# Loading every second expert tile from ScalarE's DMA queue in a mixture-of-experts decoder layer

## The chip, the cores and the metric

The kernel runs on one core of a Trainium2 chip. The metric is the device time of one execution in microseconds (us). The engines are named as in the profile: PE is TensorE's matmul, PEld its weight load, DVE VectorE, ACT ScalarE, POOL GpSimd, SP SyncE. SP computes nothing here; it issues loads and stores.

## The reference

One decoder layer for 256 tokens of width 1024 in float32. A combined projection feeds a Mamba-2 branch and a sliding-window attention branch; their gated sum is projected, added to the input and normalized to h. Then comes the part that the change touches, a layer of 32 experts of which each token uses 4:

```python
logits = xt @ w_router + b_router
top_logits, top_idx = lax.top_k(logits, 4)
gate_w = softmax(top_logits)
# for every expert e, over the tokens xb that chose it:
hgu = xb @ w_gate_up[e] + b_gate_up[e]          # (1024 x 2048) weights, 8 MB
glu, lin = split(hgu);  glu = min(glu, 7);  lin = clip(lin, -7, 7)
act = glu * sigmoid(1.702 * glu) * (lin + 1)
y   = act @ w_down[e] + b_down[e]                # (1024 x 1024) weights, 4 MB
out[t] = sum over the 4 experts of gate_w * y;   result = layer_norm(alpha * h + out)
```

## The kernel before, in words

**The stream.** All large weights are one list of 1 MB tiles, `stream` (line 85), in the order in which they are used. The first S_E = 50 belong to the projections; from there on come 32 x 12 = 384 expert tiles, which this document numbers 0 to 383. For expert e there are eight tiles "u" (gate and up weights) and four tiles "d" (down weights); the d tiles of an expert come after the u tiles of the next one (lines 177 to 183). So from e = 1 on, u of expert e are tiles 12e-4 to 12e+3, d of expert e are tiles 12e+16 to 12e+19. Each tile is read once and used for one group of matmuls.

**Buffers and the order of the loads.** A tile goes into one of NGRAN = 21 granules of 1 MB. One granule holds the normalized h (`hn`) to the end; in the expert stage the others rotate among the tiles, so that a load waits until the PE has finished the tile some 20 earlier. `weights(i)` calls `prefetch(i + 1 + st["ahead"])` (line 127), which writes the load instructions of all tiles up to `ahead` tiles further into the program, on SP. In the expert stage `ahead` is 17, and from tile 296 on (u of expert 25, line 1167) it is 6. Each load also reuses one of eight landing semaphores in turn, so it waits until the load eight before it has landed: at most eight tiles are in flight. SP executes its loads in program order and waits in front of each for its two conditions.

**One expert on the engines.** The loop at line 1159 goes over the tiles ("slots"). At each slot first the due events with pre=True run (`fire(n, True)`), then `weights`, then the tile's matmuls, then the events with pre=False. For expert e:

- after its last u tile, one slot later: ACT and DVE copy the two PSUM banks (`gu`, lines 992 and 994), the PE transposes the copies behind that slot's matmuls (`tu`, line 1004), DVE adds biases and clips, ACT takes the silu (`hg`, line 1015), DVE multiplies (`ac`). The result is needed 12 slots later;
- during the d tiles: the PE transposes gates (line 1041), ACT copies them (`S`);
- after its last d tile, one slot later: ACT copies the bank (`y`, line 1059), and behind that slot's matmuls the PE adds gates times y into the output banks (`out`, line 1054);
- for every second expert the PE gathers the token columns for two further experts in two units, and ACT copies each (`xg`).

**The branch.** After u of expert 27 (tile 327) `overflow()` (line 1063) reads a count from memory and enters a loop only if an expert has more than 64 tokens, which it has not with these inputs. Every engine takes the branch by itself.

**The end.** After tile 383 the last y and out follow, then a normalization on DVE with `lnd` (two loads of 512 KB behind the stream) and four stores. The last tile is loaded in two halves (line 105).

Of the kernel before, what the change touches and what calls it, by code (L numbers as in the profile page):

```python
# [45 lines left out]
def hybrid_layer(ctx, tc, x, w_in, conv_w, conv_b, dt_bias, a_log, d_skip, norm_w, w_ssm_out,  # L46
                 sinks, w_attn_out, b_gates, w_mix, ln1_g, ln1_b, w_router, b_router,
                 w_gate_up, b_gate_up, w_down, b_down, ln2_g, ln2_b, out, cap=CAP):
    nc = tc.nc
# [5 lines left out]
    def gtile(name, dt=F):  # L55
        return gran.tile([P, 2048], dt, name=name, tag="g")
# [39 lines left out]
    def prefetch(upto):  # L96
        while st["dma"] < min(upto, len(stream)):
            i = st["dma"]
            ap, nb = stream[i]
            t = gtile(f"raw{i}")  # L100
            t3 = t.rearrange("p (k n) -> p k n", n=nb)
            if len(halves(i)) > 1:
                nk = 2048 // nb // 2
                for k in (slice(0, nk), slice(nk, 2 * nk)):
                    nc.sync.dma_start(t3[:, k], ap[:, k])
            else:
                nc.sync.dma_start(t3, ap)  # L107
            raws[i] = t
            st["dma"] += 1

    def halves(i):

        return [slice(0, 1024), slice(1024, 2048)] if i in (0, len(stream) - 1) else [slice(0, 2048)]
# [11 lines left out]
    def weights(i):  # L125

        prefetch(i + 1 + st["ahead"])
        if i >= S_E:
            return raws.pop(i).rearrange("p (k n) -> p k n", n=1024)
        split_ahead(i)  # L130
        nb = stream[i][1]
        return tuple(t.rearrange("p (k n) -> p k n", n=nb) for t in splits.pop(i))
# [42 lines left out]
    S_E = len(stream)  # L175
# [30 lines left out]
    for c in range(2):  # L206
        nc.sync.dma_start(xn3[:, c], x[0, c * P:(c + 1) * P])
    prefetch(2)
    wdt = w1([P, KD, 32], "wdt")
    nc.sync.dma_start(wdt, w_in[0, :, OFF_DT:OFF_DT + 32].rearrange("(k p) n -> p k n", p=P))  # L210
# [692 lines left out]
    mix(1, 1)  # L903
    resid(1, 0)
    prefetch(S_E + MB)
    mix(1, 2)
    mix(1, 3)
# [326 lines left out]
```

## Time and profile before

| | |
|---|---|
| runs | 1333.29 us median of 3 (1332.5 to 1334.1) |
| profiled execution | 1332.57 us, span of the trace 1330.7 us |
| granted TensorE clock, mean | 0.988 |
| busy | PE 94%, DVE 32%, ACT 21%, POOL 5% of the span |
| DMA | 463.30 MB, mean 348 GB/s, all data loads on one queue |

Times in the rows are us from the start of the span. Busy time alone doesn't tell the bound: the rows to look at are what the PE and the load queue wait for, stage by stage. The expert stage runs from about 350 us to the end.

### The profile page before, as it was taken

To read this page: it belongs to the slowest core of one execution; us is meant where nothing else is said; L and a number is where in the kernel's file an instruction comes from. 1 tells how busy PE (TensorE), PEld (TensorE's weight loads), DVE (VectorE), ACT (ScalarE), POOL (GpSimd) and SP (SyncE) were. 2 spreads that over 40 slices of the span, in tenths; PEclk is the share of its full clock that TensorE was granted. 3 is DMA by queue.
4 is the path that set the end of the run, shared out by engine and by line. 5 is a ranking of instruction groups with operands and counts; after the bars stand their busy time and mean duration, and the time that the engine had idled before them with its cause. 6 is when DMAs were issued, how large, how long until landed. Compare 5 with 4: busy or idle time off the path is not lost. (4 is left out here: it accounts for less than half of the span.)

```text
span 1330.7 us, 16492 instructions
## 1 busy us (share of the span) xinstructions
PE 1252.8 (94%) x6864; PEld 668.4 (50%) x6864; DVE 431.6 (32%) x818; ACT 281.4 (21%) x477; POOL 63.1 (5%) x35
## 2 busy tenths in 40 slices
PE   7999999999999999999999989899898989879985
PEld 7998878999864344343342323333232323333221
DVE  6998987565632111211121111111111111111113
ACT  5555555543211111110011101001010101000001
POOL 0044332000000000000000000000000000000000
PEclk9999999999989999999999999999999999989998
DMA  9523334655999999999999999999999999989995
GB/s 300 182 64 104 118 123 147 207 185 187 355 420 421 421 421 422 421 421 420 421 421 421 422 421 420 421 421 421 421 421 421 422 421 421 421 352 421 420 420 235
DMA packets 106227, 463.30 MB, mean 348 GB/s; under 512 B 9948, under 2 KB 48996, under 8 KB 56964
## 3 DMA queue, kind: packets, MB, share of 16 engines
q1 hardware_dynamic: 106148, 462.19, 86.9%
q8 instruction: 57, 0.93, 0.3%
q14 instruction: 22, 0.18, 0.0%
HBM read 461.11 MB, written 1.05 MB: 347 GB/s over the span
## 5 line engine op out<-in xcount | busy, mean ns | idle before, releaser
L76 PE MATMUL u<-raw,xg 128*64 128x512 f32 x2048 | 470.1, 598 | 32.7 <-DMA raw<-in_w_gate_up_dram 32.6
L76 PEld LDWEIGHTS u<-raw,xg 128*64 128x64 f32 x2048 | 136.8, 136 | 335.1 <-issue 231.8
L76 PE MATMUL d<-raw,ac 128*64 128x512 f32 x1024 | 246.4, 607 | 17.6 <-DMA raw<-in_w_down_dram 11.1
L992 DVE COPY gu<-u 128x512 f32<-128x512 f32 x32 | 22.1, 692 | 708.4 <-PE u L76 708.4
L76 PEld LDWEIGHTS d<-raw,ac 128*64 128x64 f32 x1024 | 67.2, 137 | 147.0 <-issue 103.2
L65 DVE TENSOR_TENSOR wlo<-raw,whi 128x2048 fp32r<-128x2048 f32 (+1 forms) x51 | 120.4, 2371 | 13.3 <-ACT whi L62 11.4
L76 PE MATMUL ws<-xh,whi 128*128 128x256 f32 x400 | 102.1, 293 | 1.8 <-ACT whi L62 1.8
L62 ACT ACTIVATE whi<-raw 128x2048 fp32r<-128x2048 f32 (+1 forms) x51 | 95.4, 1874 | 27.6 <-DMA raw<-in_w_in_dram 8.0
L76 PE MATMUL ws<-xl,whi 128*128 128x256 f32 x400 | 98.7, 284 | 0.0
L62 ACT ACTIVATE gu<-u 128x512 f32<-128x512 f32 x32 | 19.1, 597 | 336.1 <-PE u L76 336.1
L76 PEld LDWEIGHTS ws<-xh,whi 128*128 128x128 f32 x400 | 77.2, 193 | 4.3 <-ACT whi L62 2.2
L76 PEld LDWEIGHTS ws<-xl,whi 128*128 128x128 f32 x400 | 77.3, 193 | 0.9 <-issue 0.7
L76 PEld LDWEIGHTS xg<-G,xr 128*128 128x128 f32 x512 | 62.4, 199 | 24.9 <-issue 24.3
L76 PE MATMUL xg<-G,xr 128*128 128x128 f32 x512 | 68.6, 289 | 0.2 <-DVE G L65 0.2
L62 ACT ACTIVATE xg<-xg 128x512 f32<-128x512 f32 x32 | 19.1, 597 | 216.6 <-PE xg L76 216.6
L76 PE MATMUL out<-y,S 64*128 64x512 f32 x256 | 63.6, 615 | 0.8 <-ACT y L62 0.8
L76 PE MATMUL ws<-xh,wlo 128*128 128x256 f32 x400 | 56.2, 283 | 0.0
L62 ACT ACTIVATE hg<-hg 128x512 f32<-128x512 f32 x32 | 20.2, 630 | 149.6 <-DVE hg L69 149.6
L76 PEld LDWEIGHTS ws<-xh,wlo 128*128 128x128 f32 x400 | 51.6, 192 | 0.0
L1004 PEld LDWEIGHTS tu<-ident,gu 128*128 128x128 f32 x256 | 33.2, 208 | 26.3 <-issue 25.1
L1086 POOL IOTA omisc<- 128x192 f32 x1 | 0.3, 295 | 927.4 <-DMA raw<-in_w_gate_up_dram 927.4
L76 PEld LDWEIGHTS out<-y,S 64*128 64x128 f32 x256 | 22.0, 186 | 41.9 <-issue 40.2
(249 smaller groups left out, 1171.4 us busy)
## 6 DMA issues: line engine op xcount, KB each, us to landing
raw<-in_w_gate_up_dram SPq DMA_DIRECT2D x256, 1024.0 KB, 19.8
raw<-in_w_down_dram SPq DMA_DIRECT2D x127, 1024.0 KB, 19.8
raw<-in_w_in_dram SPq DMA_DIRECT2D x33, 1024.0 KB, 5.5
raw<-in_w_ssm_out_dram SPq DMA_DIRECT2D x8, 1024.0 KB, 5.2
raw<-in_w_attn_out_dram SPq DMA_DIRECT2D x4, 1024.0 KB, 5.7
raw<-in_w_mix_out_dram SPq DMA_DIRECT2D x4, 1024.0 KB, 5.0
xn<-in_x_dram SPq DMA_DIRECT2D x2, 512.0 KB, 4.1
raw<-in_w_in_dram SPq DMA_DIRECT2D x2, 512.0 KB, 6.1
```

The source lines that it names most:

```text
L62: return nc.scalar.activation(o, i, func, **kw)
L65: return nc.vector.tensor_tensor(o, a, b, op=op)
L76: return nc.tensor.matmul(o, l, r, start=start, stop=stop)
L992: nc.vector.tensor_copy(t, banks[hf])
L1004: nc.tensor.transpose(pb[:, b], gu[hf][:, o:o + 255:2], ident)
L1086: nc.gpsimd.iota(ios, pattern=[[ns, 2], [1, ns]], base=cap, channel_multiplier=0, allow_small_or_imprecise_dtypes=True)
```

## The change

In `prefetch`, a tile that is loaded as a whole, has an odd number and is the 24th expert tile or a later one is issued by ACT instead of SP. These are tiles 25, 27, ... 381, 179 in all; tile 383 is loaded in halves and stays on SP. Nothing else is changed.

```diff
@@ prefetch
             else:
-                nc.sync.dma_start(t3, ap)
+                (nc.scalar if i % 2 and i >= S_E + 24 else nc.sync).dma_start(t3, ap)
             raws[i] = t
```

The instructions of PE, DVE and POOL stay as they were; ACT has 179 more and SP 179 fewer. Three places show how they lie. In the names, `raw_...` is the buffer of a loaded tile, `u_...` and `d_...` are PSUM banks; DMAHW0 to 7 are the landing semaphores, and a row with one of them waits there for the landing of the load that used it before.

First, ACT around the end of expert 4's u tiles (tiles 44 to 51), before; u_4447 is that expert's bank and d_4505 the bank of expert 3's d tiles (52 to 55):

```order
L62 ACTIVATE gu<-u_4309 128x512
L62 ACTIVATE hg<-hg 128x512
L62 ACTIVATE S<-S_4429 128x256
L62 ACTIVATE y<-d_4390 128x512
L62 ACTIVATE gu<-u_4447 128x512
```

The same place now, from y of expert 2 on; raw_4489 is tile 67, raw_4511 tile 69, raw_4548 tile 71, raw_4567 tile 73:

```order
L62 ACTIVATE y<-d_4390 128x512 [waits PE_49]
L107 DMA raw_4449<-in_w_gate_up_dram 128x2048 [waits DMAHW2_49]
L107 DMA raw_4465<-in_w_gate_up_dram 128x2048 [waits DMAHW4_49]
L107 DMA raw_4477<-in_w_down_dram 128x2048 [waits DMAHW6_49,PE_49]
L107 DMA raw_4489<-in_w_down_dram 128x2048 [waits DMAHW0_49,PE_49]
L62 ACTIVATE gu<-u_4447 128x512 [waits PE_49,Activation_49]
L107 DMA raw_4511<-in_w_gate_up_dram 128x2048 [waits DMAHW2_49]
L62 ACTIVATE hg<-hg 128x512 [waits DVE_49,Activation_49]
L62 ACTIVATE S<-S_4544 128x256 [waits PE_49]
L107 DMA raw_4548<-in_w_gate_up_dram 128x2048 [waits DMAHW4_49]
L62 ACTIVATE y<-d_4505 128x512 [waits PE_49]
L107 DMA raw_4567<-in_w_gate_up_dram 128x2048 [waits DMAHW6_49]
```

Four to six loads now stand between the copies of an expert: gu of tile 51 stands behind the load of tile 67, which waits for the landing of tile 59, and y of tile 55 behind the load of tile 71, which waits for tile 63.

Second, ACT where `ahead` falls from 17 to 6, now; raw_7078 is tile 311, y<-d_7035 the copy in front of tile 296's matmuls, raw_7200 tile 313 and raw_7220 tile 315:

```order
L107 DMA raw_7078<-in_w_gate_up_dram 128x2048 [waits DMAHW4_49]
L62 ACTIVATE y<-d_7035 128x512 [waits PE_49]
L62 ACTIVATE xg_7096<-xg_7109 128x4x2x64 [waits PE_49]
L62 ACTIVATE xg_7096<-xg_7131 128x4x2x64 [waits PE_49]
L62 ACTIVATE gu<-u_7092 128x512 [waits PE_49,Activation_49]
L62 ACTIVATE hg<-hg 128x512 [waits DVE_49,Activation_49]
L62 ACTIVATE S<-S_7192 128x256 [waits PE_49]
L107 DMA raw_7200<-in_w_gate_up_dram 128x2048 [waits DMAHW6_49]
L62 ACTIVATE y<-d_7157 128x512 [waits PE_49]
L107 DMA raw_7220<-in_w_gate_up_dram 128x2048 [waits DMAHW0_49]
```

Here it is the other way round: the load of tile 313 stands behind the copies of expert 25 up to S (tile 306), and tile 315 behind y of tile 307.

Third, ACT behind the branch, now; raw_7706 is tile 335, raw_7722 tile 337, raw_7742 tile 339, S_7712 belongs to tiles 328 to 331 and d_7694 is their bank:

```order
L107 DMA raw_7706<-in_w_gate_up_dram 128x2048 [waits DMAHW5_49,DMAHW4_49,DMAHW1_49]
L62 ACTIVATE S<-S_7712 128x256 [waits PE_49]
L107 DMA raw_7722<-in_w_gate_up_dram 128x2048 [waits DMAHW7_49,DMAHW6_49,DMAHW3_49]
L62 ACTIVATE y<-d_7694 128x512 [waits PE_49]
L107 DMA raw_7742<-in_w_gate_up_dram 128x2048 [waits DMAHW1_49,DMAHW0_49]
L107 DMA raw_7754<-in_w_down_dram 128x2048 [waits DMAHW3_49,DMAHW2_49]
```

SP at the same branch, now; raw_7700 is tile 334, raw_7716 tile 336, raw_7732 tile 338, raw_7748 tile 340:

```order
L1114 UNCONDITIONAL_BRANCH [waits DMAHW0_49,DMAHW1_49,DMAHW2_49,DMAHW3_49,DMAHW4_49,DMAHW5_49,DMAHW6_49,DMAHW7_49]
L107 DMA raw_7700<-in_w_gate_up_dram 128x2048 [waits DMAHW3_49,DMAHW4_49,DMAHW0_49,PE_49]
L107 DMA raw_7716<-in_w_gate_up_dram 128x2048 [waits DMAHW5_49,DMAHW6_49,DMAHW2_49,PE_49]
L107 DMA raw_7732<-in_w_gate_up_dram 128x2048 [waits DMAHW7_49,DMAHW0_49,PE_49]
L107 DMA raw_7748<-in_w_down_dram 128x2048 [waits DMAHW2_49,DMAHW1_49,PE_49]
```

SP leaves the branch when all eight landing semaphores are complete, as before, and then issues the even tiles one after the other; the odd ones come from ACT with S and y between them.

## Rows read from the trace of the kernel before

**Rows 1.** The page: the span in 40 slices, DMA share and GB/s.

```profile
DMA  9523334655999999999999999999999999989995
GB/s 300 182 64 104 118 123 147 207 185 187 355 420 421 421 421 422 421 421 420 421 421 421 422 421 420 421 421 421 421 421 421 422 421 421 421 352 421 420 420 235
```

**Rows 2.** Stretches: PE, PEld, DVE, ACT, POOL busy, PEclk, DMA share, GB/s.

```profile
500.00:600.00 100.00, 100.00 (x492) 39.08 (x488) 16.72 (x44) 11.23 (x20) 0.00 (x0) 1.00 1.01 421
...
700.00:800.00 100.00, 92.82 (x436) 33.08 (x434) 12.76 (x35) 9.02 (x16) 0.00 (x0) 1.00 1.01 421
```

**Rows 3.** SP's waits, 700 to 1100 us: total us, times, longest.

```profile
SPq L107 <- DMA raw<-in_w_gate_up_dram: 227.6, 108, 3.5
SPq L107 <- DMA raw<-in_w_down_dram: 110.4, 52, 3.5
```

**Rows 4.** SP's waits, 385 to 450 us, the longest.

```profile
SPq L107 <- PE u L76: 48.2, 22, 10.3
```

**Rows 5.** The chain that ended last: start us, us, what.

```profile
1187.72 18.15 DMA raw<-in_w_down_dram
...
1265.63 19.84 DMA raw<-in_w_gate_up_dram
...
1285.53 19.82 DMA raw<-in_w_down_dram
...
1305.49 1.94 PE d L76 x8
1307.43 1.92 PE out L76 x8
1309.35 1.87 PE d L76 x8
1311.22 0.37 PE S L1041 x2
1311.59 3.61 PE d L76 x16
```

**Rows 6.** The tile raw, 690 to 760 us: issues on SP, ns min/median/max.

```profile
L107 SPq DMA_DIRECT2D raw<-in_w_gate_up_dram x20: 327/328/328, 691.6 to 758.7; - x20
```

**Rows 7.** PE in order of time, tile 296 to 306: start us, us, what.

```profile
1094.26 1.99 PE L76 MATMUL out<-y,S 64*128 64x512 f32 x8
...
1117.71 3.85 PE L76 MATMUL d<-raw,ac 128*64 128x512 f32 x16
```

**Rows 8.** SP in order of time, 1110 to 1118 us: tile 311 on.

```profile
1109.71 7.78 SPq L107 DMA_DIRECT2D raw<-in_w_gate_up_dram  x4
```

**Rows 9.** PE in order of time around the branch and behind it.

```profile
1153.90 1.99 PE L76 MATMUL out<-y,S 64*128 64x512 f32 x8
...
1172.25 1.61 PE L1004 MATMUL tu<-ident,gu 128*128 128x128 f32 x8
1180.44 6.48 PE L76 MATMUL d<-raw,ac 128*64 128x512 f32 x16 [6.59 <-PEq L1114]
...
1187.22 3.65 PE L76 MATMUL d<-raw,ac 128*64 128x512 f32 x16
...
1192.52 1.99 PE L76 MATMUL out<-y,S 64*128 64x512 f32 x8
1194.44 12.24 PE L76 MATMUL u<-raw,xg 128*64 128x512 f32 x56
...
1211.72 3.65 PE L76 MATMUL d<-raw,ac 128*64 128x512 f32 x16
```

**Rows 10.** ACT in order of time around the branch.

```profile
1175.07 0.63 ACT L62 ACTIVATE hg<-hg 128x512 f32<-128x512 f32 x1 [2.91 <-DVE hg L69]
1187.33 0.38 ACT L62 ACTIVATE S<-S 128x256 f32<-128x256 f32 x1 [11.63 <-PE S L1041]
1190.92 0.60 ACT L62 ACTIVATE y<-d 128x512 f32<-128x512 f32 x1 [3.21 <-PE d L76]
```

**Rows 11.** SP in order of time behind the branch: tiles 334 to 339.

```profile
1184.67 2.96 SPq L107 DMA_DIRECT2D raw<-in_w_gate_up_dram  x6
```

## The prediction

> **What bounds the kernel now.** I read the page's slices first, then the stretches, then what SP and the PE wait for. From the eleventh slice on the loads move 420 to 422 GB/s with a DMA share of 9 in nearly every slice [rows 1]. The reader is to see a plateau: it doesn't follow what the PE does. Up to about 700 us the PE is busy all the time and behind the loads, later it is busy 93 of 100 us, at the same 421 GB/s [rows 2]. What SP waits for says the same: at 385 to 450 us it is the PE that must free a buffer, 48.2 us in 22 waits [rows 4]; at 700 to 1100 us it is the landing of the load eight tiles earlier, 160 waits and 338.0 us [rows 3]. Two issues eight tiles apart on the chain lie 19.90 us apart [rows 5], so a tile takes 2.49 us and the expert stage ends when the last tile has landed and the PE has done what hangs on it. One hole breaks the plateau: the slice at 1164 to 1198 us moves 352 GB/s [rows 1]. There SP waits at the branch until everything has landed and issues again at 1184.67 [rows 11].
>
> **The change part by part.** The sum is made against the profiled execution, 1332.57 us, which lies 0.72 us under the median of 1333.29. An effect of 0.2%, 2.7 us, is about what a measurement of this kernel can tell from none.
>
> *The rate.* No row shows two queues with loads at once. The 16 engines are already shown busy throughout (share 1.01 [rows 2]), so a second queue has no idle engine to fill: I take 0. For the range, 1% either way over the 900 us from tile 25 on is 9 us. The Trainium skill, "DMA: Bandwidth & Descriptors", section "Issuing engines are not separate DMA queues", speaks against the change: the loads of all issuing engines run on the same 16 DMA engines, and a second issuer saves only the issuing engine's time. The share agrees. By that rule alone the time would stay at 1333.3.
>
> *Issue time.* SP's 0.33 us of each load [rows 6] is short against 2.49 us, so nothing is gained there. ACT gets 179 x 0.33 = 59 us. It is busy 9 of 100 us [rows 2] and stays under a quarter: 0. Without that room each copy would come 0.33 us later, and the PE's next wait with it.
>
> *The wait on ACT, tiles 25 to 311.* This is new. A load that waits now stops the copies behind it. As the order shows, gu of tile 51 follows the load that waits for the landing of tile 59, and the PE needs gu behind tile 52's matmuls; y of tile 55 follows the load that waits for tile 63, and the PE needs it behind tile 56's. At both points, in every expert, the PE can't be less than seven tiles behind the landings: 7 x 2.49 = 17.4 us. While the PE is further behind anyway nothing changes; after that, where now it waits for tiles, it will wait for ACT at this distance. That costs nothing yet: a load needs the buffer of the tile 20 earlier and the landing of the one eight earlier, and when that lands the PE has finished about the fifteenth earlier. Loads stay in time: 0. If the PE fell another five tiles behind, the loads would wait for buffers.
>
> *Tiles 296 to 327.* Here `ahead` falls to 6. Tile 303 lands as the load of tile 311 goes out, 1109.7 [rows 8]; y follows (0.60), so out behind tile 296 starts at 1110.4 instead of 1094.26 [rows 7]. From there ACT's loads no longer hold the PE, and it runs freely. Its pace: with a gather, out at 1094.26 to the third d tile at 1117.71 [rows 7], and 5.30 more to the next out (1187.22 to 1192.52 [rows 9]), 28.75 us for 12 tiles; without one, 1192.52 to 1211.72 plus 5.30, 24.5 us; from out of expert 26 to the transposes after tile 327, 1153.90 to 1172.25, 18.35 us [rows 9]. So it reaches the branch at 1110.4 + 28.75 + 24.5 + 18.35 = 1182.0, 9.7 us later than before. ACT's load of tile 313, now behind S, goes out near 1134 instead of 1114.7. Four even and four odd loads in flight cover that: 0.
>
> *The branch.* SP leaves it when tile 333 has landed, which the loads decide and not the PE: 1184.7 as before, 0 with some 1 us either way. The PE is through at 1180.4 + 9.7 = 1190.1.
>
> *Behind the branch.* SP issues 334, 336, 338 and 340 in a row. ACT is past its silu at 1175.70 + 9.7 = 1185.4 [rows 10] and issues 335; but 337 stands behind S and 339 behind y, 1187.33 and 1190.92 before [rows 10], 9.7 us later now. The pace after the pause: tile 340, the seventh, landed at 1205.87 [rows 5], 21.2 us after 1184.67, so 3.8 us to start and 2.49 each. Tiles 334 and 335 land by 1193.5. The load of 337 goes out at 1187.33 + 0.38 + 9.7 = 1197.4 and joins 2.3 to 3.8 us later, at 1199.7 to 1201.2. In between SP's queue has all the engines and lands about three even tiles. From there each queue gets half, an estimate, since both always have work and no row prefers either: 4.97 us a tile. That lead of the even tiles never goes back. 337 lands at 1204.7 to 1206.2, 379 at 1309.1 to 1310.6, 381 at 1314.1 to 1315.6, while SP ends with 382 and 383 and loads `lnd`. The Trainium skill, same page, section "Queues, rings and completion order", says that an engine takes turns between the queues that have work, packet by packet; no run here shows that, and it would give the half.
>
> *The end.* Before, the PE finished tile 383 at 1315.2 [rows 5]. Now it waits for 379, then does 379 (1.94), 380 (1.87), out (1.92), 381 (1.87), S (0.37) and 382 with 383 (3.61) [rows 5]: 11.6 us after 379, 1320.7 to 1322.2. That is 5.5 to 7.0 us more. I take 6, nearer the early joining, since engines that are already running need no start.
>
> The bounds of this term: 0, if the lead doesn't arise; and the lead the buffers allow. A tile 20 ahead of the PE is the last that may be issued, four even loads in flight cover eight tiles, so even tiles land at most 12 ahead. Then six odd ones are left, 371 at 1303.1 to 381 at 1315.5, and the PE still has 13 tiles with their rest: five u at 1.72 (12.06 for seven [rows 9]) and, from the rows named, about 18.5 us, together 27.2: 1330.3, or 15 us more.
>
> Sum: 1333.29 + 6 = 1339.3 us.
>
> **The rivals.**
>
> *The PE reaches the branch early.* If it catches up faster, or is never held back, ACT passes the branch at 1176 and issues 335 while SP still waits for landings. That tile fills the hole, worth up to 2.49 us, and 337 and 339 follow in time; no lead arises, no tail: 1330.8 to 1333.3. It decides where the 9.7 us shrink to about 3: then 337 goes out at 1187.7 + 3 = 1190.7 and joins as 335 lands at 1193.5. Against it is the sum of 9.7; for it, that an expert takes the PE 28.75 or 24.5 us free of waits against 29.8 of loading, so it has something to spare in every one. Chance 0.22.
>
> *A faster rate.* Two queues might close small pauses between loads. With 1%: -9 + 6, 1330.3. The share of 1.01 speaks against it. Chance 0.08.
>
> *More lead, or late loads.* If ACT's queue gets less than half, or its copies are late more often and its loads with them, the lead grows to the buffers' bound, or the rate falls by 1%: +9 to +15, 1342 to 1348. For it is that every odd load stands behind a copy that waits for the PE; against it, four loads in flight. Chance 0.20.
>
> That the change does nothing is out: the order shows 179 loads moved.
>
> **How the numbers follow.** Forecast 0.50, its own range 1336 to 1342. The range from 1330.5 to 1347 leaves out the far end of the faster rate and of the larger lead. Slower by over 0.2%: 0.47 of the forecast and 0.19 of the third rival, 0.66. Within 0.2%: 0.19 of the first rival, 0.03 of the forecast, 0.01 of the second and 0.01 of the third, 0.24. Faster: 0.07 and 0.03, 0.10.
>
> **What would show it.** In the profile after, ACT's waits at line 107 for landings should be hundreds of us; the PE at 700 to 1100 us should wait for gu and y from ACT, not for tiles, with 421 GB/s unchanged. SP should issue again behind the branch at about 1184.7, the PE start at about 1190. At the end the PE should wait for odd tiles, and SP's queue be empty before ACT's. A rate other than 421, a hole in it at 700 to 1100 us, or a PE at the branch before 1178 would make the prediction wrong.

## The result and the profile after

The changed kernel takes 1342.87 us (median of 4, 1342.09 to 1343.8), the kernel before 1332.89 us beside it (median of 4): ratio 1.0072, 95% interval 1.0059 to 1.0085, 10.0 us slower. That lies in the range; the forecast was 1339.3. The profiled execution took 1342.47 us, span 1340.7. PE finishes tile 383 at 1325.1 instead of 1315.2 (the sums of the last rows of the two chains), so all of the loss lies ahead of that point.

The page: the slices of [rows 1] again, and the two load queues (q1 is SP's, q10 is ACT's).

```profile
GB/s 295 184 64 109 112 126 157 197 201 177 381 421 395 422 420 421 420 421 421 420 422 422 421 421 420 421 421 421 421 421 421 422 421 411 419 309 421 420 421 182
...
q1 hardware_dynamic: 80372, 274.48, 52.6%
q10 hardware_dynamic: 25776, 187.71, 33.8%
```

The plateau is as high as before, 421, with two queues instead of one. It is lower in three places: 395 at 402 to 436 us, 411 at 1106 to 1139, and 309 at 1173 to 1207, where the pause at the branch lies (352 before).

Stretches of the kernel before, then of the one after (PE, PEld, DVE, ACT, POOL busy, PEclk, DMA share, GB/s):

```profile
390.00:440.00 50.00, 50.00 (x238) 19.83 (x232) 8.41 (x24) 5.51 (x10) 0.00 (x0) 1.00 1.01 421
...
1100.00:1140.00 40.00, 37.16 (x175) 12.89 (x176) 3.98 (x10) 3.40 (x6) 0.29 (x1) 1.00 1.01 421
1140.00:1180.00 40.00, 32.29 (x162) 13.38 (x158) 8.54 (x23) 4.63 (x8) 0.00 (x0) 0.95 0.99 411
1180.00:1220.00 40.00, 38.97 (x166) 13.16 (x168) 4.38 (x12) 3.19 (x6) 0.00 (x0) 0.92 0.92 375
```

```profile
390.00:440.00 50.00, 50.00 (x230) 19.67 (x228) 8.17 (x22) 5.16 (x10) 0.00 (x0) 0.97 0.98 403
...
1100.00:1140.00 40.00, 35.90 (x172) 15.00 (x170) 7.40 (x20) 5.01 (x9) 0.00 (x0) 0.91 1.01 413
1140.00:1180.00 40.00, 40.00 (x194) 14.52 (x188) 4.38 (x12) 3.40 (x6) 0.29 (x1) 1.00 0.96 397
1180.00:1220.00 40.00, 36.22 (x170) 14.03 (x169) 5.36 (x15) 3.40 (x6) 0.00 (x0) 0.96 0.86 351
```

At 421 GB/s the missing bytes are worth 18/421 x 50 = 2.1 us at the start, 0.8 us, 1.3 us and 2.3 us: 6.5 us of loads that come later. The first of these differs between executions: a kernel with the same program up to tile 333 (to_branch, below) moved 417 GB/s there, 0.5 us.

In between the PE is held by ACT. ACT's waits at 700 to 1100 us, and the PE's:

```profile
ACT gu L62 <- DMA raw<-in_w_gate_up_dram: 134.1, 10, 19.4
...
ACT hg L62 <- DMA raw<-in_w_gate_up_dram: 43.7, 10, 4.6
ACT y L62 <- DMA raw<-in_w_gate_up_dram: 40.3, 10, 5.0
```

```profile
PE tu L1004 <- ACT gu L62: 24.4, 6, 4.1
PE out L76 <- ACT y L62: 4.1, 4, 2.1
```

The PE waits for no tile there. One such place in ACT's order, and in the PE's behind it:

```profile
858.56 5.31 ACTq L107 DMA_DIRECT2D raw<-in_w_down_dram  x2
863.97 0.60 ACT L62 ACTIVATE gu<-u 128x512 f32<-128x512 f32 x1 [19.39 <-DMA raw<-in_w_gate_up_dram]
```

```profile
864.62 1.98 PE L1004 MATMUL tu<-ident,gu 128*128 128x128 f32 x8 [4.10 <-ACT gu L62]
```

The copy gu can't go before the two loads ahead of it have gone, the second of which waits for a landing; the transposes start 0.65 us after the copy does.

The branch. SP in order of time (before: 1184.67 [rows 11]), then ACT:

```profile
1190.20 1.62 SPq L107 DMA_DIRECT2D raw<-in_w_gate_up_dram  x3
```

```profile
1182.32 0.60 ACT L62 ACTIVATE xg<-xg 128x512 f32<-128x512 f32 x1 [6.69 <-PE xg L76]
1182.33 0.33 ACTq L107 DMA_DIRECT2D raw<-in_w_down_dram  x1
1182.70 0.85 ACTq L107 DMA_DIRECT2D raw<-in_w_gate_up_dram  x1
...
1191.24 0.34 ACTq L107 DMA_DIRECT2D raw<-in_w_gate_up_dram  x1
1198.21 0.38 ACT L62 ACTIVATE S<-S 128x256 f32<-128x256 f32 x1 [7.24 <-PE S L1041]
1198.30 0.34 ACTq L107 DMA_DIRECT2D raw<-in_w_gate_up_dram  x1
1201.81 0.60 ACT L62 ACTIVATE y<-d 128x512 f32<-128x512 f32 x1 [3.21 <-PE d L76]
1201.87 0.33 ACTq L107 DMA_DIRECT2D raw<-in_w_gate_up_dram  x1
```

Tiles 331 and 333 stand behind the second gather copy, which waits for the late PE: they go out at 1182.33 and 1182.70 and land at 1187.1 and 1189.6, while SP's last tile, 332, landed at 1173.8. SP leaves when 333 has landed, 5.5 us later than before. Behind the branch 335, 337 and 339 go out at 1191.24, 1198.30 and 1201.87.

The end of the chain, beside [rows 5]:

```profile
1251.43 3.76 PE d L76 x16
1255.22 18.86 DMA raw<-in_w_gate_up_dram
...
1275.41 18.63 DMA raw<-in_w_gate_up_dram
1294.06 19.56 DMA raw<-in_w_down_dram
1313.67 3.65 PE d L76 x16
...
1321.48 3.61 PE d L76 x16
```

The loads are the odd tiles 363, 371 and 379, from ACT; 379 lands at 1313.6. SP's even tiles are ahead of them: 380, which is needed after 379, landed at 1309.4. Ahead of 363 the chain is the PE's own work from the branch on (1192.78), up to d at 1251.43; then ACT copies it (y, at 1255.21), and the load of 363 goes out right behind that copy. SP's late leaving is not on this chain: the late PE is, and ACT's order, which ties 363 to it.

### The profile page after: what moved, and what is told of

Read it like the earlier page. It is cut to its first block, busy times and chain, and to the rows that moved or that the text cites. A ratio compares the mean times of both kernels' runs of the same rounds, so it can differ in the third digit from the quotient of the medians.

```text
span 1340.7 us, 16359 instructions
## 1 busy us (share of the span) xinstructions
PE 1252.1 (93%) x6864; PEld 680.2 (51%) x6864; DVE 432.5 (32%) x818; ACT 280.3 (21%) x477; POOL 60.1 (4%) x35
## 5 line engine op out<-in xcount | busy, mean ns | idle before, releaser
L76 PE MATMUL u<-raw,xg 128*64 128x512 f32 x2048 | 461.9, 597 | 7.8 <-DMA raw<-in_w_gate_up_dram 7.8
L76 PEld LDWEIGHTS u<-raw,xg 128*64 128x64 f32 x2048 | 141.2, 137 | 294.6 <-issue 241.2
L76 PE MATMUL d<-raw,ac 128*64 128x512 f32 x1024 | 251.8, 625 | 5.3 <-DVE gg L70 3.7
L76 PEld LDWEIGHTS d<-raw,ac 128*64 128x64 f32 x1024 | 70.4, 142 | 133.8 <-issue 116.9
L62 ACT ACTIVATE gu<-u 128x512 f32<-128x512 f32 x32 | 19.1, 597 | 361.3 <-DMA raw<-in_w_gate_up_dram 221.0
L1004 PE MATMUL tu<-ident,gu 128*128 128x128 f32 x256 | 45.4, 328 | 40.6 <-ACT gu L62 40.4
L1004 PEld LDWEIGHTS tu<-ident,gu 128*128 128x128 f32 x256 | 37.4, 212 | 67.5 <-ACT gu L62 55.1
L62 ACT ACTIVATE xg<-xg 128x512 f32<-128x512 f32 x32 | 19.1, 597 | 210.4 <-PE xg L76 157.5
L65 DVE TENSOR_TENSOR hg<-tu,bgu 128x256 f32<-128x256 f32 x64 | 26.9, 421 | 82.3 <-PE tu L1004 81.4
```

Of the source, the lines that this page charges most:

```text
L62: return nc.scalar.activation(o, i, func, **kw)
L65: return nc.vector.tensor_tensor(o, a, b, op=op)
L76: return nc.tensor.matmul(o, l, r, start=start, stop=stop)
L1004: nc.tensor.transpose(pb[:, b], gu[hf][:, o:o + 255:2], ident)
```

## The experiments

Where a landing is named, it is the time at which the last of a tile's 16 engines reported in the trace. Ratios are against runs of the kernel before on the same chip. Of each edit only the expression that picks the issuing engine is printed.

**lag_only.** ACT has the odd tiles 25 to 311 and nothing later.

```diff
-nc.scalar if i % 2 and i >= S_E + 24 else nc.sync
+nc.scalar if i % 2 and S_E + 24 <= i < S_E + 312 else nc.sync
```

> Only tiles 25 to 311, odd, go out from ACT; from tile 312 on every load is on SP again. My theory (ACT's program order does it: it holds the PE back, which by itself is covered, and costs where late copies make the loads behind them late, at the branch and behind it): the PE still runs 17 to 25 us behind the landings at 600 to 1100 us with the clock falling after its waits, and ends tile 327 near 1187; SP leaves the branch at 1184.7 + 1.4 (the loss after tile 25); the PE then runs freely to the end. 1.5 to 3.5 us over before. Rival (two queues cost by themselves, or the lag does): 6 to 10 us over before.

1334.14 us, ratio 1.0012 [1.0003, 1.0021], 1.3 us slower. PE at 700 to 1100 us, SP at the branch, and the PE's stretch behind it:

```profile
PE tu L1004 <- ACT gu L62: 25.6, 6, 4.8
```

```profile
1185.35 2.99 SPq L107 DMA_DIRECT2D raw<-in_w_gate_up_dram  x6
```

```profile
1200.00:1300.00 100.00, 100.00 (x478) 36.54 (x475) 13.54 (x35) 9.40 (x17) 0.00 (x0) 1.00 1.01 421
```

The PE comes to the branch as late as with the whole change (tile 327 done at 1186.2; 1187.6 there, 1172.3 before), yet SP leaves at 1185.35, and the PE is done at 1316.2. The lag alone is nearly free (a little less than the theory's 1.5 us; the rival's 6 to 10 are out), but it has used up what the PE had to spare: from its transposes at 1186.09 the PE works 130.1 us to its end without waiting for a tile, where before it took 142.9 us from 1172.25. In this kernel the end is set by the PE, and a later PE would end later.

**before_branch.** ACT has 313 to 333 alone.

```diff
+nc.scalar if i % 2 and S_E + 312 <= i < S_E + 334 else nc.sync
```

> Only tiles 313 to 333, odd, go out from ACT. My theory: without the lag the copies in front of these loads come in time, tile 331 goes out near 1168 and SP leaves the branch at 1184.7 to 1185.5: 0 to 1 us over before. Rival (a load behind a copy is late in any case): 331 goes out late, a hole before the branch, 3 to 6 us over before.

1333.38 us, ratio 1.0001 [0.9992, 1.0010]. SP left at 1184.63: no loss without the lag.

**behind_branch.** ACT has 335 to 381 alone.

```diff
+nc.scalar if i % 2 and i >= S_E + 334 else nc.sync
```

> Only tiles 335 to 381, odd, go out from ACT. My theory: without the lag tiles 337 and 339 go out at about 1188 and 1192 instead of 1198 and 1202, the even tiles get a lead of at most one tile, and the end is 0 to 2 us later. Rival (the lead comes from the two queues and the copies by themselves): the same tail as with the whole change, 4 to 6 us over before. Third possibility: ACT issues 335 while SP still waits at the branch, and it is 2 us faster.

1334.45 us, ratio 1.0014 [1.0005, 1.0023], 1.6 us slower. ACT's first load, tile 335:

```profile
1184.33 0.38 ACTq L107 DMA_DIRECT2D raw<-in_w_gate_up_dram  x1
```

ACT was done with its silu at 1175.6, but the load went out 0.25 us after tile 333 had landed (1184.07). So a load on ACT doesn't fill the pause at the branch here, as the rival of the early PE had it.

These three parts sum to +3.3 us by their medians; the whole is +10. The rest is in how they act together.

**short_distance.** The whole change, with `ahead` lowered to 7 from expert 12 on, so that ACT's loads need not wait for landings.

```diff
+            if kind == "u" and e == 12:
+                st["ahead"] = 7
```

> The whole change, but from tile 140 on (u of expert 12) the loads stand 7 tiles ahead in the program instead of 17, so that ACT's loads wait for landings that are long past. My theory: the PE's lag shrinks from 20 us at 700 us to a few us by 1000 us, ACT's waits for landings at L107 go, the clock stays at full, the branch is reached in time; what is left is the loss after tile 25 and some of the tail: 2 to 5 us over before. Rival (two queues cost by themselves): 8 to 10 us, as the whole change.

1337.87 us, ratio 1.0044 [1.0030, 1.0058], 5.0 us slower. PE at 700 to 1100 us:

```profile
PE u L76 <- DMA raw<-in_w_gate_up_dram: 17.2, 15, 1.3
```

The waits for gu are gone and the PE waits for tiles again, as in the kernel before. SP left the branch at 1184.82, and PE's end came at 1319.8: SP's late leaving and half of the loss are gone, the other half stayed and lies behind the branch. The lag itself went only in part, against the expectation: the PE's transposes behind tile 327 came at 1181.1, 8.9 us late. The shorter distance pulled the queues apart: tile 301 landed 9.7 us later than before, tile 300 7.9 us earlier.

**from_313.** No lag, and all later odd tiles on ACT (before_branch and behind_branch together).

```diff
+nc.scalar if i % 2 and i >= S_E + 312 else nc.sync
```

> Only the odd tiles 313 to 381 are issued by ACT, so the PE reaches the branch without the lag that tiles 25 to 311 build up, and all loads near the branch and behind it stand on ACT as in the whole change. Theory A (the lag is needed for the loss): ACT's 335 goes out at 1184 to 1186, 337 by 1189, 339 by 1192.5, sum +1 to +3.5 us (1334 to 1336.5). Rival C (ACT's place in the order behind the branch costs whether the PE is late or not): 339 lands after 1208 and the sum is +6 us or more (1339 and up).

1335.91 us, ratio 1.0018 [1.0009, 1.0027], 2.7 us slower; 335, 337 and 339 went out at 1183.3, 1190.4 and 1194.0, the last two 1.5 us behind what A expected. Without the lag 2.7 of the 10 us are left, so most of the loss needs it.

**to_branch.** The whole change up to tile 333, SP alone behind the branch.

```diff
+nc.scalar if i % 2 and S_E + 24 <= i < S_E + 334 else nc.sync
```

> Only the odd tiles 25 to 333 are issued by ACT, SP has all tiles behind the branch. Theory A: SP leaves the branch at 1189 to 1191 as with the whole change, the stretch from there to the PE's end is 130.5 us as before, sum +4 to +6.5 us (1337 to 1339.5). Rival B (what is lost at the branch is won back behind it, and the tail alone costs): +0 to +3 us.

1338.64 us, ratio 1.0046 [1.0033, 1.0060], 5.7 us slower; SP at the branch:

```profile
1190.17 2.49 SPq L107 DMA_DIRECT2D raw<-in_w_gate_up_dram  x4
```

It leaves as late as with the whole change, 5.5 us, and PE's end comes 5.5 us later (1320.7): behind the branch nothing is won back and nothing is lost, and the chain that ended last is SP's loads all the way from there. With lag_only this places the loss: nearly the same lag (transposes at 1187.5 and 1186.1) costs 1.3 us when SP has 313 to 333, 5.7 us when ACT has them.

**three_back.** The whole change, with 329, 331 and 333 on SP.

```diff
+nc.scalar if i % 2 and i >= S_E + 24 and i not in (S_E + 329, S_E + 331, S_E + 333) else nc.sync
```

> The whole change, but tiles 329, 331 and 333 are issued by SP. Theory A (the 5.5 us late at the branch come from 331 and 333 standing behind the late copy of the gathered columns on ACT): SP leaves the branch at 1185 to 1187 instead of 1190.2, the tail stays as long as with the whole change, sum +5 to +7.5 us (1338 to 1340.5). Rival B (the PE's own lag of 15 us at tile 327 makes the branch late whoever issues these tiles): SP leaves at 1189 or later, sum +9 to +10.5 us (1342 to 1343.5).

1342.48 us, ratio 1.0074 [1.0060, 1.0088], as slow as the whole change. SP, and ACT's 337 with the copy ahead of it:

```profile
1186.34 1.59 SPq L107 DMA_DIRECT2D raw<-in_w_gate_up_dram  x3
```

```profile
1201.04 0.38 ACT L62 ACTIVATE S<-S 128x256 f32<-128x256 f32 x1 [10.12 <-DMA raw<-in_w_down_dram]
1201.12 0.33 ACTq L107 DMA_DIRECT2D raw<-in_w_gate_up_dram  x1
```

Theory A had SP's leaving right, rival B the time; neither had the mechanism. SP left 3.9 us earlier, but ACT's next loads did not: they hang on the PE through S and y (the row of S names a landing, but the PE's own S ended at 1201.0, just ahead of it), and 339 went out at 1204.70. The time won went to even tiles only, while the chain that ended last runs through the PE and a load behind an ACT copy, as in the whole change. The runs are not alike in one more thing: from transposes at the same time (1187.46 and 1187.52) the PE began behind the branch at 1195.38 here and at 1192.78 there. Those 2.6 us lie on that chain, and no run shows where they come from.

**six_back.** 329 to 339 on SP.

```diff
+nc.scalar if i % 2 and i >= S_E + 24 and not S_E + 329 <= i < S_E + 340 else nc.sync
```

> The whole change, but the six odd tiles next to the branch, 329 to 339, are issued by SP. When only 329, 331 and 333 were given back, SP left the branch at 1186.3, yet 335, 337 and 339 still stood behind hg, S and y of the late PE on ACT (1191.2, 1201.1, 1204.7) and the end did not move. Theory A, as mended by that (what costs is the issue of the odd tiles on both sides of the branch, held by ACT's copies while the PE is 15 us late): SP leaves at 1185 to 1187 and loads 334 to 340 without a pause, 341 stands behind y at about 1204 but is not needed in the queue before 1208, the sum is +3 to +5.5 us (1336 to 1338.5). Rival B (the PE's 15 us by themselves set the end, since it works without a pause behind the branch): the PE's end at 1323 to 1326 as with the whole change, sum +9 to +10.5 us (1342 to 1343.5).

1341.23 us, ratio 1.0065 [1.0051, 1.0078], 8.0 us slower, nearer to rival B, whose end of the PE held (1324.8). But B's cause is out by lag_only, where the same late PE ended at 1316.2. The two queues at 1215 to 1255 us (packets, MB, share), and the issues (median us to landing):

```profile
q1 hardware_dynamic: 1277, 9.30, 55.9%
q10 hardware_dynamic: 1031, 7.53, 45.3%
...
raw<-in_w_gate_up_dram ACTq DMA_DIRECT2D x5, 1024.0 KB, 11.8
raw<-in_w_gate_up_dram SPq DMA_DIRECT2D x5, 1024.0 KB, 17.7
```

ACT's queue, q10, is short of loads: each lands 11.8 us after its issue, where a full queue took 17.7 on SP. It falls further behind, though DMA never idles.

**What the kernels so far have in common** is how far the two queues stand apart. In one queue tile 361 lands 2.49 us after 360. The gap is what 361 - 360 departs from that; the later of the two tiles comes late by the mean delay plus half the gap.

| kernel | 360 lands | 361 lands | mean delay | gap | later tile | PE's end |
|---|---|---|---|---|---|---|
| before | 1255.62 | 1258.11 | | 0 | | 1315.17 |
| lag_only | 1256.27 | 1258.74 | +0.6 | 0 | +0.6 | +1.0 |
| before_branch | 1256.09 | 1258.57 | +0.5 | 0 | +0.5 | +0.5 |
| behind_branch | 1257.39 | 1259.71 | +1.7 | -0.2 | +1.8 | +1.8 |
| to_branch | 1261.14 | 1263.62 | +5.5 | 0 | +5.5 | +5.5 |
| from_313 | 1255.05 | 1260.83 | +1.1 | 3.3 | +2.7 | +1.8 |
| short_distance | 1254.44 | 1263.92 | +2.3 | 7.0 | +5.8 | +4.6 |
| whole change | 1259.72 | 1269.12 | +7.6 | 6.9 | +11.0 | +9.9 |
| three_back | 1249.76 | 1271.32 | +3.7 | 19.1 | +13.2 | +9.9 |
| six_back | 1251.24 | 1270.06 | +3.8 | 16.3 | +12.0 | +9.6 |

PE's end follows the later tile, less 1 to 3 us where there is a gap: at the very end the trailing queue catches up (in three_back tile 371 lands 13.6 us late and 379 only 7.0, as SP's even tiles run out), and then the PE's own work sets the end. The table shows that the two go together; that the gap is a cause of its own is argued from it. three_back and six_back halved the mean delay and more than doubled the gap.

**gpsimd_queue.** Is it ACT's order, or two queues as such? The whole change with POOL, which has no copies to make, in ACT's place.

```diff
+nc.gpsimd if i % 2 and i >= S_E + 24 else nc.sync
```

> The whole change, but the odd tiles 25 to 381 are issued by POOL, which has no other work in the expert stage. Theory A (ACT's program order: a load that waits for its buffer or its semaphore holds back the copies behind it, the copies hold back the PE, and the loads behind the copies come late): with POOL the PE never waits 4 us for gu, ends tile 327 at 1172 to 1177 as before, SP leaves the branch by 1186, and the sum is +0 to +4 us (1333 to 1337). Rival B (two queues by themselves: sharing makes the odd tiles late whoever issues them): PE waits for tiles in 700 to 1100 or an end that is +8 to +11 us, as with ACT (1341 to 1344). A third outcome, that a queue fed by POOL is slower than 4.97 us a tile, would show in the bytes per slice (below 421 GB/s).

1335.11 us, ratio 1.0019 [1.0010, 1.0028], 2.2 us slower. PE at 700 to 1100 us, and the end of the chain:

```profile
PE u L76 <- DMA raw<-in_w_gate_up_dram: 22.8, 22, 1.3
```

```profile
1219.34 39.69 DMA raw<-in_w_gate_up_dram
...
1298.93 1.94 PE d L76 x8
```

No wait for gu, hardly a lag, and 419 and 421 GB/s in the two slices around the branch: POOL issued 335 at 1156 and filled the pause. Theory A's numbers hold (tile 327 done at 1174.3, SP left at 1183.96): four fifths of the 10 us are gone. A second thing changed beside ACT's order: POOL's loads have landing semaphores of their own, so each queue has eight tiles in flight instead of four. That the PE no longer waits for gu is the order, since no load stands ahead of the copies now; how much of the four fifths the deeper queues bring wasn't separated. That the pause was filled and 2.2 us are lost all the same is again the gap: 361 (POOL) landed at 1253.8 and 360 (SP) at 1259.0, 7.7 us apart the other way; SP's tiles trail, 39.7 us from issue to landing, eight at 4.96.

**gpsimd_branch.** The kernel before with 332 and 333 on POOL.

```diff
-nc.sync.dma_start(t3, ap)
+(nc.gpsimd if i in (S_E + 332, S_E + 333) else nc.sync).dma_start(t3, ap)
```

> The kernel before, with tiles 332 and 333 alone issued by POOL, so that SP has to await only tile 331 in front of the branch and can issue tile 334 while 332 and 333 still flow. If the hole behind the branch (one queue empty from the landing of 333 to the first bytes of 334) is what costs: SP leaves at 1179 to 1181 instead of 1184.7, the PE's end comes 2 to 4 us earlier (1329 to 1331). If SP's leaving is bound by the PE or by its own buffers there: 1184 and no change (1332 to 1334). If POOL's two loads come late as ACT's did: later than before by up to 3 us.

1334.06 us, ratio 1.0010 [1.0001, 1.0019]: no gain. SP left at 1184.35. POOL issued its two loads at 1134.1 and 1136.6, as soon as their buffers were free, and they landed at 1144.0 and 1149.0, ahead of some fifteen tiles that are needed sooner. SP's queue came 4.5 us later for it (320 landed at 1156.4 instead of 1151.9), and the pause stayed: 343 GB/s in its slice (352 before).

**gpsimd_over_branch.** The kernel before with the odd tiles 313 to 339 on POOL.

```diff
+(nc.gpsimd if i % 2 and S_E + 312 <= i < S_E + 340 else nc.sync).dma_start(t3, ap)
```

> The kernel before, with the odd tiles 313 to 339 issued by POOL, whose queue holds loads that still flow while SP's is drained in front of the branch (with POOL for all odd tiles, 335 was issued at 1156 and landed at 1187.8). If the pause behind the branch is what costs: the slice from 1165 to 1200 moves about 420 GB/s instead of 340, every later tile lands up to 4 us earlier, the PE's end at 1311 to 1313 instead of 1315.2 and the time 1329 to 1331. If sharing between two queues costs as much as the pause (with POOL throughout, +2.2 us): 1332 to 1335.

1338.82 us, ratio 1.0040 [1.0026, 1.0053], 5.6 us slower; neither expectation held. The loads do gain: 360 lands at 1253.4, 2.2 us earlier than before. But POOL issued 313 at 1088.6, when SP was at 302; 313 landed at 1098.6 and 312 at 1154.9 instead of 1132.0. The PE waited for SP's tiles, finished tile 327 at 1192.5, 20 us late, and the rest is its own work, 129 us to 1321.5 without waiting for a tile (busy 99.49 of the 100 us from 1200 to 1300). Queues that stand apart in front of the branch hold the PE as well.

**gpsimd_tail.** The lag, then SP for 329 to 339, then POOL.

```diff
+nc.gpsimd if i % 2 and i >= S_E + 340 else nc.scalar if i % 2 and S_E + 24 <= i < S_E + 329 else nc.sync
```

> The odd tiles 25 to 327 are issued by ACT (so the PE comes to the branch some 15 us late, as in the whole change), 329 to 339 by SP, and 341 to 381 by POOL, which has no copies to make. With ACT for 341 to 381 the sum was +8.0 us, the odd tiles 341 to 361 landing every 5.5 us and the even ones every 4.5. Theory A (ACT's loads behind the branch go out one behind each copy of the late PE, so that its queue runs short): POOL's loads go out earlier than ACT's did, 361 lands before 1266 instead of 1270, the PE's end at 1316 to 1320, sum +1.5 to +4.5 us (1335 to 1338). Rival B (two queues behind a late PE give uneven landings whoever issues): 361 at 1268 to 1272, the PE's end at 1323 to 1326, sum +7 to +10 us (1340 to 1343.5).

1341.11 us, ratio 1.0061 [1.0047, 1.0074], 7.7 us slower: rival B's time. The chain:

```profile
1218.51 39.71 DMA raw<-in_w_gate_up_dram
```

This is one of SP's tiles, and so is the next on the chain, at 1258.29. The experiment did not take away the gap but turned it round: POOL started at 341 at 1184.2, while SP had 334 to 340 still ahead of it. 361 landed at 1250.3, 360 at 1268.2, a gap of 20.3 us with the even tiles 12.5 us late and PE's end 8.1 us late. So A's first number held (361 before 1266) and its time didn't.

No version beat the kernel before. One that fills the pause without letting a queue run ahead would need POOL's loads to be held back; it wasn't tried. The 2.2 us by which 360 landed early in gpsimd_over_branch are all that a run shows of such a gain.

## Why the prediction was right in sign, and where it was wrong

**Rate and issue time** held: 421 GB/s with either, 0.33 us per load on ACT. By the section "Issuing engines are not separate DMA queues" of the Trainium skill's "DMA: Bandwidth & Descriptors" alone the time would have stayed at 1333.3. The rate agrees with it; the 10 us come from ACT's program order and the queues' uneven places.

**The wait on ACT** held as a mechanism: at 700 to 1100 us the PE waits for gu and y and for no tile. By itself the late PE has a small price, +1.3 us in lag_only.

**Loads stay in time: 0** failed in part. At the stage's end the loads were 2.9 us late (mean of 303 and 304, which landed at 1114.07 and 1113.44 against 1109.64 and 1112.13), 2.1 us of it by the row at 390 to 440, and 303 another 1.5 us by half a gap. So y, behind the load of 311, was copied by 1115.07, and out could not start at the predicted 1110.4. It started at 1115.91: the PE had worked without a wait from 1104.72 on, at first at the lower clock (last section), which makes the last 0.8 us. The price of the clock is a term that the prediction doesn't have. From there the free run of 71.6 us was right, and the PE's transposes behind tile 327 came at 1187.5, not at 1182.0.

**Tiles 296 to 327, 0, and the branch, "which the loads decide and not the PE", 0 with some 1 us**: this is the step that failed. SP left 5.5 us later. Four loads in flight on each queue don't cover it where an odd load stands behind a gather copy: 331 and 333 waited for the PE, and SP for 333. to_branch has this term and the lag without anything behind the branch (5.7 us), lag_only has the lag without the term (1.3 us), and before_branch these loads on ACT without the lag (0.5 us, not told from none).

**Behind the branch and the end, 6 us** was right in kind and a little large: from SP's leaving to PE's end it is 134.9 us against 130.5, 4.4 us. On the prediction's own chain, 337 went out at 1198.30 (1197.4 predicted) but landed at 1208.3 instead of 1204.7 to 1206.2, among SP's tiles 336 to 340, which SP had sent 5.5 us later; 379 landed at 1313.6 instead of 1309.1 to 1310.6, and the PE ended 11.4 us behind it (11.6 predicted). One sign of the prediction was wrong, that SP's queue would be empty before ACT's: 383 landed at 1318.4, 381 at 1317.4. Each queue had half; the two at 1225 to 1265 us:

```profile
q10 hardware_dynamic: 1155, 8.41, 50.6%
q1 hardware_dynamic: 1147, 8.35, 50.4%
```

That even share fits the turn-taking that the section "Queues, rings and completion order" of the Trainium skill's "DMA: Bandwidth & Descriptors" describes; no run shows its grain. The lead that "never goes back" is the gap of the table.

**The rivals.** The early PE did not come about, and behind_branch shows that its gain was none: ACT's 335 went out at 1184.3, not 1176. The faster rate is out. "Late loads" had the right thought, that an odd load stands behind a copy that waits for the PE; the time lies 0.9 us above that rival's lower end and 3.6 us above the forecast. But what that rival priced, a lead that grows to the buffers' bound or a lower rate, did not come: the gap was 6.9 us. So the time lies 0.9 us outside the forecast's own range of 1336 to 1342, and within the whole range for a reason that no rival priced. The sum was 6, measured 10: along time 5.5 up to SP's leaving, which had been set to 0, and 4.4 from there on. These are not two causes that can be taken away one by one: three_back won 3.9 of the 5.5 back and ended no earlier, since the chain that ended last runs through the PE and ACT's copies.

**What is open.** In the whole change 1 us of the mean delay has no stretch of its own. How much of the loss behind the branch is ACT's order and how much the start from uneven places wasn't separated by an experiment: gpsimd_tail changed both. The trace of the whole change shows that ACT's order is at work: its loads 347 to 363 went out 2.0 to 7.9 us after the tile eight before had landed, with the copies ahead of them, and SP's 348 to 362 within 0.1 us. It was also not tried to keep the lag and the gap at 0 with two queues.

## What to carry to other kernels

A load on an engine that also computes stands in its program order both ways: its wait holds back the copies behind it, and the copies hold back the loads behind them; a lag that costs little by itself can so make the next drain late. And two queues that both have work and share the engines evenly kept their distance here (in the whole change the odd tiles were some 4 us behind their place from tile 101 to tile 301): half of it is what the trailing one's tiles come late on top of the mean delay, so look at when neighbouring tiles land, not at the bytes per second, which show nothing. Moving single loads back to the first queue, or on to a free one, only moved the distance in these runs.

## What the runs showed of the hardware

The granted clock fell after short pauses of the PE. Stretches of the kernel after, around the wait of 4.10 us at 864.62 (PEclk is third from the end):

```profile
840.00:864.00 24.00, 20.52 (x95) 6.49 (x90) 1.63 (x4) 0.63 (x2) 0.00 (x0) 1.00 1.01 421
864.00:868.00 4.00, 3.38 (x12) 2.11 (x14) 2.12 (x6) 0.57 (x1) 0.00 (x0) 0.57 1.02 424
868.00:872.00 4.00, 4.00 (x20) 1.26 (x18) 1.16 (x4) 1.01 (x2) 0.00 (x0) 1.00 1.00 418
```

0.57 over these 4 us means mostly the 1.2 GHz level, in the first 4 us of work after the pause; eight transposes took 1.98 us, 1.61 at the full clock. The kernel before idles 7 us in the 100 us of [rows 2], in waits for tiles of at most 0.6 us each, at a clock of 1.00. There the PE was held by ACT again 60 us later, so it cost nothing that the runs show. Behind the last such wait, 4.11 us at 1104.72, it did:

```profile
1104.00:1110.00 6.00, 5.28 (x16) 2.35 (x16) 2.54 (x7) 1.23 (x2) 0.00 (x0) 0.50 1.03 425
```

```profile
1106.63 3.68 PE L76 MATMUL d<-raw,ac 128*64 128x512 f32 x8
...
1115.91 1.99 PE L76 MATMUL out<-y,S 64*128 64x512 f32 x8
```

```profile
1114.47 0.60 ACT L62 ACTIVATE y<-d 128x512 f32<-128x512 f32 x1 [3.37 <-PE d L76]
```

From the transposes at 1104.72 to out at 1115.91 the PE took 11.19 us without a wait, with the clock at the 1.2 GHz level up to 1110; one expert later, from 1135.98 to 1144.67 at a clock of 1.00, the same work took 8.69 us. y was ready at 1115.07, so out could have started 0.8 us earlier; that much of the PE's lag at the branch is the clock's.
